# Attention: another order of query tiles and half-head preparation, one pool of three transpose banks, samples' scores half a quarter later

## The chip, the cores and the metric

The kernel runs on one core of one Trainium2 chip. The metric is device time in microseconds (us) of one execution. A run is timed several times and the median is given; beside it one execution is profiled, and its trace gives the engines' instructions with their start and length. The engines are PE (matrix), DVE (vector), ACT (scalar), POOL and SP; SP only issues transfers here. "Clock" is the granted clock of PE as a share of its full speed.

## What is computed

One layer of a streaming encoder for a prompt of 1024 tokens and for 8 samples of 16 tokens, each sample with its own 1024 cached keys and values.

```python
# prompt x (1, 1024, 1024), samples x (8, 16, 1024) with 1024 cached keys and values each
N_HEADS, HEAD_DIM, V_DIM, CHUNK = 4, 64, 128, 64          # a head has two maps of 64
h = rmsnorm(x, g_mix); z = h @ w_in
zq, zk, zv, zu = jnp.split(z, [QK_COLS, 2 * QK_COLS, 2 * QK_COLS + ATTN_WIDTH], axis=-1)
q, k = rmsnorm(zq per map, g_q), rmsnorm(zk per map, g_k)
k_all, v_all = concatenate([k_past, k]), concatenate([v_past, v])
def diff_attend(q, k, v, bias, mask, lam):
    s = jnp.einsum('bqhmd,bkhmd->bhmqk', q, k).astype(jnp.float32) * (HEAD_DIM ** -0.5)
    s = jnp.where(mask, s + bias[None, :, None], NEG_INF)
    p = jax.nn.softmax(s, axis=-1)
    w = p[:, :, 0] - lam * p[:, :, 1]
    return jnp.einsum('bhqk,bkhe->bqhe', w.astype(v.dtype), v)
# the prompt: block-causal, in query tiles of 128; the samples: 16 queries over 1024 + 16 keys.
# o is normalised per head, joined to the depthwise convolution's half (GLU, 31 taps, LayerNorm,
# swish) and projected by w_out; then memory cross-attention and an MLP of 4096, both with residuals
```

## The kernel before

All of the prompt's input projections come first, to about 293 us of the span. Then comes the **attention stage**, from the last `z` matmul at 293.0 us to 538.33 us, where the first matmul of the output projection `pj` starts. Cross-attention and the MLP follow. The change touches only the attention stage.

In the stage four generators, the streams, issue work and are woven into one program:

- `prompt_stream`: for each of 4 heads, 8 query tiles of 128 rows. `attend` computes a tile's scores. For each of two maps and each bank of 512 keys it issues two matmuls, one with the rounded queries `qs` (L674) and one with their rest `ql` (L675), into a bank `sc`. A reduction on DVE (L679) moves the bank to `p` and finds its extreme, ACT takes the exponential (L681), and DVE mixes both maps (L688). `values` transposes the mixed weights (`pT`, L699), copies them to `wT` (L701, in turn by ACT and DVE) and multiplies by the values into `po` (L704). Tile i has i + 1 blocks of 128 keys.
- `prep(h, c)` makes half c (512 rows) of head h ready: two loads `r`, four transposes of keys (`kst`, L619) and four of queries (`qst`), two copies by ACT and two by DVE that split keys into `kS` (L628, L629), and four and two for `qs`, `ql` (L639 to L641). Tile 0 to 3 of a head need half 0; tiles 4 to 7 need both halves' keys and half 1's queries.
- `sample_stream`: for each sample four quarters of 256 cached keys. For a quarter, eight transposes in two groups of four (two heads each, in the bank `kT`, L768), each group copied by ACT to `ku` (L770), then four score matmuls `ss` (L777), one for each head, on 32 columns of the array each. Then come the exponential `sp` (L800), the transposes `wt` (L810) and the values `spo` (L825), and ACT's copy `raw` (L830).
- `conv_norm` and `memory_stream`: the conv's normalisation (`cvt`, `cvT`) and the memory's keys and values (`memT`, `mk`, `mv`).

A program orders each engine's instructions when the kernel is built, by the streams' progress, by priorities and by its own estimate of when inputs are ready. On the chip each engine then runs its list in order. The eight PSUM banks are pools by tag: a transpose that takes a bank waits until the bank's last user has been read. The next stage's banks for `pj` take the place of the samples' banks, so `pj` starts only after the last sample. The prompt's last tiles may run beside it.

The lines that set the order before are these:

```python
PA = 3
PB1 = {"sc": 2, "tr": 2, "po": 1, "kT": 1, "ss": 1, "acc": 1}
if i % 4 == PA and n + 4 - PA < len(tiles):
    its.append(prep(tiles[n + 4 - PA][0], tiles[n + 4 - PA][1] // 4))
```

So the next half is prepared beside tile 3 (or 7), one tile ahead of its first use.

Of the kernel before, what the change touches and what calls it, by code (L numbers as in the profile page):

```python
# [10 lines left out]
F32 = mybir.dt.float32  # L11
R32 = mybir.dt.float32r
AF = mybir.ActivationFunctionType
ALU = mybir.AluOpType
# [26 lines left out]

EL = 3

PA = 3


NS, NL = 4, 3
# [6 lines left out]
TRS = ("tr", "sc", "tr", "sc", "kT", "sx")  # L54
WP, WS, WL, WM = (0, 1), (0, 1), (.2, .8), (.2, .8)
AB = {"rq": 2, "kS": 2, "rv": 4, "qs": 2, "p": (3, 1), "wT": 2}
PB1 = {"sc": 2, "tr": 2, "po": 1, "kT": 1, "ss": 1, "acc": 1}


def f32(ap):  # L60
# [4 lines left out]
def kernel(  # L65
# [489 lines left out]

    p2 = ExitStack()
    ppt = {}
    for nm, tags in (("ppsS", ("kT", "ss", "acc")), ("ppsP", ("sc", "tr", "po"))):
        pl = p2.enter_context(tc.tile_pool(name=nm, bufs=1, space=PSUM, reuse_waits="tile"))
        ppt.update({t: pl for t in tags})  # L560
    wlm = p2.enter_context(tc.tile_pool(name="wkM", bufs=1, side="right", reuse_waits="tile"))
# [60 lines left out]
    def prep_keys(h, c):  # L622

        ps = flipped(halves[1, h, c], f"kst{h}_{c}")
        kS = wk.tile([P, 2, 512], R32, name=f"kS{h}_{c}", tag="kS", bufs=AB["kS"])
        kSs.setdefault(h, []).append(kS)
        for m in range(2):
            act.copy(kS[HALF[m], m, :], ps[HALF[m]])  # L628
            dve.tensor_sub(kS[HALF[1 - m], m, :], ps[HALF[m]], f32(kS[HALF[m], m, :]))  # L629
        yield  # L630

    def prep_queries(h, c):

        ps = flipped(halves[0, h, c], f"qst{h}_{c}")
        qs = wk.tile([P, 2, 512], R32, name=f"qs{h}_{c}", tag="qs", bufs=AB["qs"])
        ql = qlow[c]
        for m in range(2):
            a, b = HALF[m], HALF[1 - m]
            act.activation(qs[a, m, :], ps[a], AF.Copy, scale=gqk[a])  # L639
            act.activation(qs[b, m, :], ps[a], AF.Copy, scale=gqk[a])  # L640
            dve.scalar_tensor_tensor(out=ql[a, m, :], in0=ps[a], scalar=gqk[a], in1=f32(qs[a, m, :]),  # L641
                                     op0=ALU.mult, op1=ALU.subtract)
        qss[h, c] = (qs, ql)
        yield
# [74 lines left out]
    def prompt_stream():  # L719
        for c in range(2):  # L720
            qlow.append((wk1 if c else wk).tile([P, 2, 512], R32, name=f"ql{c}", bufs=1))
            pool.memset(f32(qlow[c]), 0.0)
        tiles = [(h, i) for h in range(NH) for i in range(8)]
        yield from prep(0, 0)
        last = iter(())
        for n, (h, i) in enumerate(tiles):
            st = {}
            its = [attend(h, i, st), last]
            if i % 4 == PA and n + 4 - PA < len(tiles):
                its.append(prep(tiles[n + 4 - PA][0], tiles[n + 4 - PA][1] // 4))  # L730
            yield from alternate(*its)
            last = values(h, i, st["w"], st["s0"])
        yield from last
# [4 lines left out]
    def sample_setup():  # L738
        for wi in range(2):
            r = rpool.tile([P, 512], F32, name=f"n8_{wi}", tag="r")  # L740
            sp.dma_start(r, d8[wi])
            ps = bk("kT", f"t8_{wi}")
            for h in range(NH):
                pe.transpose(ps[:, h * P:(h + 1) * P], r[:, h * P:(h + 1) * P], ident)
            if wi:
# [6 lines left out]

    def sample_keys(b):

        pm = ws.tile([P, 1152], F32, name=f"sp{b}", tag="sp", bufs=2)
        mn = [3e38]
        for c in range(2):
            sb = bk("ss", f"ss{b}_{c}")
            for cc in range(2):
                if (b, 2 * c + cc) not in krs:  # L760
                    load_keys(b, 2 * c + cc)
                kr = krs[b, 2 * c + cc]
                u = ws.tile([P, NH, 256], F32, name=f"ku{b}_{c}_{cc}", tag="ku", bufs=UB)
                for hp in range(2):
                    ps = bk("kT", f"kT{b}_{c}_{cc}_{hp}")
                    for h in range(2):
                        for t in range(2):
                            pe.transpose(ps[:, h * 256 + t * P:h * 256 + (t + 1) * P],  # L768
                                         kr[:, t, (2 * hp + h) * P:(2 * hp + h + 1) * P], ident)
                    act.copy(u[:, 2 * hp:2 * hp + 2, :], ps.rearrange("p (h k) -> p h k", h=2))  # L770
                    yield
                with tc.high_priority(offset=TILED):

                    hs = (2, 3, 0, 1)
                    for n, h in enumerate(hs):
                        with tc.issue_after(lead) if n else ExitStack():
                            i = pe.matmul(sb[32 * h:32 * h + 32, cc * 256:cc * 256 + 256], zq[:, b, h, :], u[:, h, :],  # L777
                                          start=True, stop=True)
                        lead = lead if n else i.ins
                    sx["lead"] = lead  # L780
                if cc:
                    init, mn[0] = mn[0], sm(1, "smn", bufs=8)
                    add = biass if c else zero.broadcast_to([P, 512])
                    dve.tensor_tensor_reduce(out=pm[:, c * 512:(c + 1) * 512], in0=sb, in1=add, scale=1.0, scalar=init,
                                             op0=ALU.add, op1=ALU.min, accum_out=mn[0])
                yield
        sx["sc", b] = (pm, mn[0])

    def sample_weights(b):
# [44 lines left out]
    def sample_stream():  # L834
        sample_setup()
        yield from sample_keys(0)
        for b in range(8):
# [3 lines left out]
                continue  # L841

            vals = sample_values(b)
            for n, _ in enumerate(sample_keys(b + 1)):
                if n % 3 == 2:
                    next(vals)
                yield

# [815 lines left out]
```

## Time and profile before

| | |
|---|---|
| Median of 3 runs | 1572.34 us (1572.21 to 1577.45) |
| The profiled execution | 1569.38 us, of which the span is 1567.6 |
| PE busy in the span | 1496.2 us, 95% |
| DVE, ACT, POOL busy | 1094.0, 731.4, 297.8 us |
| Mean granted clock | 0.99 |
| Attention stage | 293.0 to 538.33 us of the span |

The profiled execution is 3.0 us under the median; 1.8 us of it lie outside the span. Times in rows count from the span's start. A row with "x4" stands for four records; a matmul of `po`, `ss` or `spo` leaves two records, one of `sc` or a transpose one. A busy share says how full an engine was, not that it was the limit; where PE sits idle, the row names the instruction whose end let it go on.

### The profile page before, as it was taken

What the parts mean: (1) busy time and instruction counts of PE and PEld (TensorE: products, weight loads), DVE (VectorE), ACT (ScalarE), POOL (GpSimd) and SP (SyncE); (2) the same over time, 40 slices, a digit from 0 to 9 for tenths busy, and PEclk for the clock granted to TensorE, in tenths of its full rate; (3) what the DMA queues carried; (4) which work ended last, traced back from release to release, by engine and by line L of the source; (5) the groups of instructions that cost most, each with busy time, mean ns of one, the idle gap of its engine ahead of it and who ended that gap; (6) DMA issues with size and microseconds to landing.
All of it is one profiled execution on the core that took longest, in us unless ns stands there. A gap on an engine that the chain in (4) does not pass through costs nothing.

```text
span 1567.6 us, 25652 instructions
## 1 busy us (share of the span) xinstructions
PE 1496.2 (95%) x9326; PEld 1293.3 (83%) x9326; DVE 1094.0 (70%) x1984; ACT 731.4 (47%) x1530; POOL 297.8 (19%) x410
## 2 busy tenths in 40 slices
PE   7999989888899899999999999999999999999999
PEld 7989787666677688886678999999999788878887
DVE  5999999975657754535758786666566556996565
ACT  6312011386777742634656454444353444544442
POOL 5354682032545330231011000000000000000000
PEclk9999999899999999999999999999999999999999
DMA  6423242567776553012422554443474567744443
GB/s 202 143 83 101 85 137 99 176 201 240 237 239 217 181 206 108 28 48 96 139 103 89 179 185 145 162 160 121 160 235 140 167 206 227 238 126 110 124 135 95
DMA packets 187122, 237.88 MB, mean 152 GB/s; under 512 B 23851, under 2 KB 101717, under 8 KB 186996
## 3 DMA queue, kind: packets, MB, share of 16 engines
q1 hardware_dynamic: 186996, 236.25, 47.2%
q8 instruction: 73, 1.20, 0.3%
q14 instruction: 53, 0.43, 0.1%
HBM read 172.59 MB, written 63.60 MB: 151 GB/s over the span
## 4 chain that ended last, share of the span: by engine, by line
PE 66%; DVE 7%; ACT 5%; DMA 5%; issue 2%; POOL 1%; SPq 0%; DVEq 0%; ACTq 0%; POOLq 0%
PE p L124 13%; PE p L123 13%; PE p L125 13%; PE pj L123 3%; PE pj L124 3%; PE pj L125 3%; DVE acc L307 1%; PE po L704 1%; PE q L124 1%; PE q L123 1%; PE q L125 1%; PE kT L768 1%; PE z L124 1%; PE z L125 1%; PE z L123 1%
## 5 line engine op out<-in xcount | busy, mean ns | idle before, releaser
L124 PE MATMUL p<-Bp,Ap 128*128 128x512 f32 x448 | 175.0, 391 | 1.1 <-DVE Bp L1532 1.1
L125 PE MATMUL p<-Bp,Ap 128*128 128x512 f32 x448 | 174.4, 390 | 0.0
L307 DVE SCALAR_TENSOR_TENSOR acc<-cp,wc,acc 128x1024 f32<-128x1024 f32 (+2 forms) x150 | 167.3, 1117 | 1.2
L123 PE MATMUL p<-Bp,Ap 128*128 128x512 f32 x448 | 158.1, 390 | 3.9 <-ACT Bp L1531 2.9
L1531 ACT CAST Ap<-w_xb 128x512 fp32r<-128x512 f32 x112 | 69.5, 621 | 161.8 <-PE p L125 131.7
L1532 DVE TENSOR_TENSOR Ap<-w_xb,Ap 128x512 fp32r<-128x512 f32 x112 | 76.9, 687 | 91.3 <-ACT Ap L1531 91.2
L123 PE MATMUL p<-b_t,s 128*128 128x288 f32 x384 | 114.5, 298 | 2.8 <-ACT s L1284 2.8
L124 PE MATMUL p<-b_t,s 128*128 128x288 f32 x384 | 114.4, 298 | 0.0
L125 PE MATMUL p<-b_t,s 128*128 128x288 f32 x384 | 113.9, 298 | 0.0
L123 PEld LDWEIGHTS p<-Bp,Ap 128*128 128x128 f32 x448 | 84.0, 188 | 22.3 <-ACT Bp L1531 3.8
L124 PEld LDWEIGHTS p<-Bp,Ap 128*128 128x128 f32 x448 | 84.1, 188 | 20.2 <-DVE Bp L1532 3.0
L125 PEld LDWEIGHTS p<-Bp,Ap 128*128 128x128 f32 x448 | 84.1, 188 | 17.4
L124 PE MATMUL z<-wqkv,h 128*128 128x512 f32 x216 | 85.7, 397 | 1.3 <-DVE wqkv L116 1.1
L123 PE MATMUL z<-wqkv,h 128*128 128x512 f32 x216 | 86.1, 399 | 0.0
L125 PE MATMUL z<-wqkv,h 128*128 128x512 f32 x216 | 85.4, 395 | 0.0
L123 PE MATMUL p<-b_b,a 128*128 128x288 f32 x256 | 75.9, 297 | 0.0
L124 PE MATMUL p<-b_b,a 128*128 128x288 f32 x256 | 75.7, 296 | 0.0
L125 PE MATMUL p<-b_b,a 128*128 128x288 f32 x256 | 75.6, 296 | 0.0
L123 PEld LDWEIGHTS p<-b_t,s 128*128 128x128 f32 x384 | 72.8, 190 | 3.3 <-ACT s L1284 3.3
L1368 ACT ACTIVATE o<-o 128x576 f32<-128x576 f32 x64 | 43.8, 685 | 68.1 <-DVE o L1378 29.2
L1051 DVE TENSOR_TENSOR XP<-pj,XP 128x512 f32<-128x512 f32 x54 | 37.1, 688 | 52.4 <-PE pj L125 52.2
L124 PEld LDWEIGHTS p<-b_t,s 128*128 128x128 f32 x384 | 73.0, 190 | 0.0
(513 smaller groups left out, 4315.9 us busy)
## 6 DMA issues: line engine op xcount, KB each, us to landing
kr<-in_cache_k_dram SPq DMA_DIRECT2D x32, 512.0 KB
vu<-in_cache_v_dram SPq DMA_DIRECT2D x32, 512.0 KB
w1t<-in_w_ff_dram SPq DMA_DIRECT2D x32, 512.0 KB
w_xb<-ds SPq DMA_DIRECT2D x64, 256.0 KB
da<-o SPq DMA_DIRECT2D x48, 256.0 KB
w_xb<-da SPq DMA_DIRECT2D x48, 256.0 KB
ds<-o SPq DMA_DIRECT2D x32, 256.0 KB
dxr<-XP SPq DMA_DIRECT2D x18, 256.0 KB
```

Of the source, the lines that this page charges most:

```text
L123: pe.matmul(out, lh, rh, start=first, stop=False)
L124: pe.matmul(out, lh, rl, start=False, stop=False)
L125: pe.matmul(out, ll, rh, start=False, stop=last)
L307: dve.scalar_tensor_tensor(out=out, in0=cp[:, lo + j:hi + j], scalar=wj, in1=out, op0=ALU.mult, op1=ALU.add)
L704: pe.matmul(po, wT[:, j * P:(j + 1) * P], vss[h][jb][:, j], start=4 * jb + j == 0, stop=4 * jb + j == i)
L768: pe.transpose(ps[:, h * 256 + t * P:h * 256 + (t + 1) * P], kr[:, t, (2 * hp + h) * P:(2 * hp + h + 1) * P], ident)
L1051: dve.tensor_add(xr[t][n], ps, xr[t][n])
L1368: act.activation(c, c, AF.Relu)
L1531: act.copy(u[:, 0], src)
L1532: dve.tensor_sub(u[:, 1], src, f32(u[:, 0]))
```

## The change

1. **Tiles.** Heads 0 to 2 take their query tiles in the order `QO` = 0, 1, 4, 5, 6, 7, 2, 3; head 3 keeps 0 to 7. Half 1 of a head is prepared beside its first tile, and half 0 of the next head beside the seventh in order. Buffers of `kS`, `qs` and `ql` go by the parity of head plus half, one each.
2. **Banks.** The bank `kT` is gone; `tr` has three banks in place of two, and the samples' key transposes take them too.
3. **Samples.** `sample_keys` issues a quarter's scores after the first group of the next quarter's transposes. The second group's copy is made by DVE in place of ACT (32 of 64 copies).

```diff
@@ -41,7 +41,7 @@
 EL = 3
-PA = 3
+QO = (0, 1, 4, 5, 6, 7, 2, 3)
@@ -54,7 +54,7 @@
 WP, WS, WL, WM = (0, 1), (0, 1), (.2, .8), (.2, .8)
 AB = {"rq": 2, "kS": 2, "rv": 4, "qs": 2, "p": (3, 1), "wT": 2}
-PB1 = {"sc": 2, "tr": 2, "po": 1, "kT": 1, "ss": 1, "acc": 1}
+PB1 = {"sc": 2, "tr": 3, "po": 1, "ss": 1, "acc": 1}
@@ -555,7 +555,7 @@
     p2 = ExitStack()
     ppt = {}
-    for nm, tags in (("ppsS", ("kT", "ss", "acc")), ("ppsP", ("sc", "tr", "po"))):
+    for nm, tags in (("ppsS", ("ss", "acc")), ("ppsP", ("sc", "tr", "po"))):
         pl = p2.enter_context(tc.tile_pool(name=nm, bufs=1, space=PSUM, reuse_waits="tile"))
         ppt.update({t: pl for t in tags})
@@ -622,7 +622,7 @@
         ps = flipped(halves[1, h, c], f"kst{h}_{c}")
-        kS = wk.tile([P, 2, 512], R32, name=f"kS{h}_{c}", tag="kS", bufs=AB["kS"])
+        kS = wk.tile([P, 2, 512], R32, name=f"kS{h}_{c}", tag=f"kS{(h + c) % 2}", bufs=1)
         kSs.setdefault(h, []).append(kS)
         for m in range(2):
@@ -632,8 +632,8 @@
         ps = flipped(halves[0, h, c], f"qst{h}_{c}")
-        qs = wk.tile([P, 2, 512], R32, name=f"qs{h}_{c}", tag="qs", bufs=AB["qs"])
-        ql = qlow[c]
+        qs = wk.tile([P, 2, 512], R32, name=f"qs{h}_{c}", tag=f"qs{(h + c) % 2}", bufs=1)
+        ql = qlow[(h + c) % 2]
         for m in range(2):
             a, b = HALF[m], HALF[1 - m]
@@ -720,14 +720,16 @@
             qlow.append((wk1 if c else wk).tile([P, 2, 512], R32, name=f"ql{c}", bufs=1))
             pool.memset(f32(qlow[c]), 0.0)
-        tiles = [(h, i) for h in range(NH) for i in range(8)]
+        tiles = [(h, i) for h in range(NH) for i in (QO if h < NH - 1 else range(8))]
         yield from prep(0, 0)
         last = iter(())
...
             st = {}
             its = [attend(h, i, st), last]
-            if i % 4 == PA and n + 4 - PA < len(tiles):
-                its.append(prep(tiles[n + 4 - PA][0], tiles[n + 4 - PA][1] // 4))
+            if n % 8 == 0:
+                its.append(prep(h, 1))
+            elif n % 8 == 6 and h < NH - 1:
+                its.append(prep(h + 1, 0))
             yield from alternate(*its)
             last = values(h, i, st["w"], st["s0"])
@@ -739,7 +741,7 @@
             r = rpool.tile([P, 512], F32, name=f"n8_{wi}", tag="r")
             sp.dma_start(r, d8[wi])
-            ps = bk("kT", f"t8_{wi}")
+            ps = bk("tr", f"t8_{wi}")
             for h in range(NH):
                 pe.transpose(ps[:, h * P:(h + 1) * P], r[:, h * P:(h + 1) * P], ident)
@@ -752,38 +754,52 @@
     def sample_keys(b):
+
         pm = ws.tile([P, 1152], F32, name=f"sp{b}", tag="sp", bufs=2)
-        mn = [3e38]
-        for c in range(2):
-            sb = bk("ss", f"ss{b}_{c}")
-            for cc in range(2):
-                if (b, 2 * c + cc) not in krs:
-                    load_keys(b, 2 * c + cc)
-                kr = krs[b, 2 * c + cc]
-                u = ws.tile([P, NH, 256], F32, name=f"ku{b}_{c}_{cc}", tag="ku", bufs=UB)
-                for hp in range(2):
-                    ps = bk("kT", f"kT{b}_{c}_{cc}_{hp}")
-                    for h in range(2):
-                        for t in range(2):
-                            pe.transpose(ps[:, h * 256 + t * P:h * 256 + (t + 1) * P],
-                                         kr[:, t, (2 * hp + h) * P:(2 * hp + h + 1) * P], ident)
-                    act.copy(u[:, 2 * hp:2 * hp + 2, :], ps.rearrange("p (h k) -> p h k", h=2))
-                    yield
-                with tc.high_priority(offset=TILED):
-
-                    hs = (2, 3, 0, 1)
-                    for n, h in enumerate(hs):
-                        with tc.issue_after(lead) if n else ExitStack():
-                            i = pe.matmul(sb[32 * h:32 * h + 32, cc * 256:cc * 256 + 256], zq[:, b, h, :], u[:, h, :],
-                                          start=True, stop=True)
-                        lead = lead if n else i.ins
-                    sx["lead"] = lead
-                if cc:
-                    init, mn[0] = mn[0], sm(1, "smn", bufs=8)
-                    add = biass if c else zero.broadcast_to([P, 512])
-                    dve.tensor_tensor_reduce(out=pm[:, c * 512:(c + 1) * 512], in0=sb, in1=add, scale=1.0, scalar=init,
-                                             op0=ALU.add, op1=ALU.min, accum_out=mn[0])
-                yield
+        mn, us, sbs = [3e38], [], []
+
+        def transposes(j, hp):
+            if (b, j) not in krs:
+                load_keys(b, j)
+            if not hp:
+                us.append(ws.tile([P, NH, 256], F32, name=f"ku{b}_{j}", tag="ku", bufs=UB))
+            ps = bk("tr", f"kT{b}_{j}_{hp}")
+            for h in range(2):
+                for t in range(2):
+                    i = pe.transpose(ps[:, h * 256 + t * P:h * 256 + (t + 1) * P],
+                                     krs[b, j][:, t, (2 * hp + h) * P:(2 * hp + h + 1) * P], ident)
+            (dve.tensor_copy if hp else act.copy)(us[j][:, 2 * hp:2 * hp + 2, :], ps.rearrange("p (h k) -> p h k", h=2))
+            return i.ins
+
+        def scores(j, lead):
+            c, cc = divmod(j, 2)
+            if not cc:
+                sbs.append(bk("ss", f"ss{b}_{c}"))
+            with tc.high_priority(offset=TILED):
+
+                for h in range(NH):
+                    with tc.issue_after(lead):
+                        i = pe.matmul(sbs[c][32 * h:32 * h + 32, cc * 256:cc * 256 + 256], zq[:, b, h, :], us[j][:, h, :],
+                                      start=True, stop=True)
+                    if not h:
+                        lead = i.ins
+            sx["lead"] = lead
+            if cc:
+                init, mn[0] = mn[0], sm(1, "smn", bufs=8)
+                add = biass if c else zero.broadcast_to([P, 512])
+                dve.tensor_tensor_reduce(out=pm[:, c * 512:(c + 1) * 512], in0=sbs[c], in1=add, scale=1.0, scalar=init,
+                                         op0=ALU.add, op1=ALU.min, accum_out=mn[0])
+
+        for j in range(4):
+            lead = transposes(j, 0)
+            yield False
+            if j:
+                scores(j - 1, lead)
+                yield True
+            lead = transposes(j, 1)
+            yield False
+        scores(3, lead)
+        yield True
         sx["sc", b] = (pm, mn[0])
@@ -841,8 +857,8 @@
             vals = sample_values(b)
-            for n, _ in enumerate(sample_keys(b + 1)):
-                if n % 3 == 2:
+            for scored in sample_keys(b + 1):
+                if scored:
                     next(vals)
                 yield
```

**Where instructions move.** The first place is PE where head 0 ends and head 1 begins: `sc_2`, `sc_3` and `sc_0` are scores of query tiles 2, 3 and 0, `r_1_0` a loaded half of head 1. Before:

```order
L768 MATMUL kT_0_0_0_4032<-ident,kr_0_4029 128x128 x4
L619 MATMUL qst_0_3509<-ident,r_1_0_3426 128x128 x4
L794 MATMUL ss_2_3885<-k_917,zq 32x128 x4
L582 MATMUL cvt_3524<-ident,al_3525 128x128 x4
L768 MATMUL kT_0_0_1_4072<-ident,kr_0_4029 128x128 x4
L674 MATMUL sc_0_0_0_3585<-kS_0_3435,qs_0_3514 128x128
L675 MATMUL sc_0_0_0_3585<-kS_0_3435,ql_2748 128x128
```

After:

```order
L675 MATMUL sc_3_1_0_3562<-kS_0_2758,ql_2747 128x512
L782 MATMUL ss_1_3272<-ku_3_3252,zq 32x256 x2
L582 MATMUL cvt_3356<-ident,al_3357 128x128 x4
L810 MATMUL ss_2_3411<-k_917,zq 32x128 x4
L704 MATMUL po_7_3302<-vr_0_2751,wT_7_0_3308 128x128 x4
L881 MATMUL memT_0_3376<-ident,mem_3374 128x128 x4
L881 MATMUL memT_1_3389<-ident,mem_3374 128x128 x4
L826 MATMUL wt_0_3440<-ident,sp_3063 128x128 x4
L619 MATMUL qst_0_3424<-ident,r_1_0_3312 128x128 x4
L826 MATMUL wt_4_3458<-ident,sp_3063 128x128 x4
L826 MATMUL wt_8_3515<-ident,sp_3063 128x128
L674 MATMUL sc_0_0_0_3609<-kS_0_3321,qs_0_3429 128x128
```

Before, the keys' transposes `kst` stand twenty rows above this piece, and no score of the prompt lies between them and `sc_0_0_0`. After, they stand just above the first row shown, and scores of tile 3 (`sc_3_1_0`) follow them, with only `qst` and other streams' pieces before `sc_0_0_0`.

The second place is PE at the end of the attention stage; `spo` on `v_918` is the last sample's last product. Before:

```order
L699 MATMUL pT_3_0_6142<-ident,p_3_0_6004 128x128 x4
L704 MATMUL po_2_6011<-vr_0_5568,wT_2_0_6016 128x128 x3
L825 MATMUL spo_6362<-vu_6_6429,wt_6298 32x128 x8
L825 MATMUL spo_6362<-v_918,wt_6298 32x128 x4
L674 MATMUL sc_4_1_0_6156<-kS_0_5575,qs_1_6079 128x512
L675 MATMUL sc_4_1_0_6156<-kS_0_5575,ql_2750 128x512
L674 MATMUL sc_4_1_1_6161<-kS_1_6044,qs_1_6079 128x128
L675 MATMUL sc_4_1_1_6161<-kS_1_6044,ql_2750 128x128
L123 MATMUL pj_0_6603<-wo_4_6565,MT_6552 128x512
L124 MATMUL pj_0_6603<-wo_4_6565,MT_6552 128x512
L123 MATMUL pj_0_6619<-wo_4_6565,MT_6552 128x512
L124 MATMUL pj_0_6619<-wo_4_6565,MT_6552 128x512
```

After:

```order
L699 MATMUL pT_7_1_6506<-ident,p_7_0_6417 128x128
L841 MATMUL spo_6362<-vu_6_6429,wt_6298 32x128 x8
L841 MATMUL spo_6362<-v_918,wt_6298 32x128 x4
L704 MATMUL po_7_6494<-vr_0_5524,wT_7_0_6500 128x128 x4
L704 MATMUL po_7_6494<-vr_1_5815,wT_7_1_6511 128x128 x4
L123 MATMUL pj_0_6603<-wo_4_6565,MT_6552 128x512
L124 MATMUL pj_0_6603<-wo_4_6565,MT_6552 128x512
L123 MATMUL pj_0_6619<-wo_4_6565,MT_6552 128x512
L124 MATMUL pj_0_6619<-wo_4_6565,MT_6552 128x512
```

Before, scores of head 3's tiles 4 and 5 stand around the first `pj`, and 24 score matmuls of its tiles 5 to 7, 26 transposes `pT` and 30 matmuls `po` of the prompt follow it. After, the prompt's last product `po_7` stands ahead of the first `pj`.

The third place is PE at a quarter's sample scores, early in head 1 (before, `ku_0_0` is a sample's quarter 0 and `kT_0_1` its quarter 1; after, `ku_3` is quarter 3). Before:

```order
L768 MATMUL kT_0_0_1_4587<-ident,kr_0_4574 128x128 x4
L699 MATMUL pT_3_0_4093<-ident,p_3_0_3896 128x128 x4
L674 MATMUL sc_4_0_0_4081<-kS_0_3435,qs_1_4020 128x512
L674 MATMUL sc_4_0_1_4086<-kS_1_3980,qs_1_4020 128x128
L675 MATMUL sc_4_0_0_4081<-kS_0_3435,ql_2750 128x512
L675 MATMUL sc_4_0_1_4086<-kS_1_3980,ql_2750 128x128
L810 MATMUL wt_0_4431<-ident,sp_4027 128x128 x4
L777 MATMUL ss_0_4573<-ku_0_0_4576,zq 32x256 x4
L768 MATMUL kT_0_1_0_4658<-ident,kr_1_4655 128x128 x4
L704 MATMUL po_3_4092<-vr_0_3428,wT_3_0_4098 128x128 x4
```

After:

```order
L769 MATMUL kT_3_1_3829<-ident,kr_3_3782 128x128 x4
L674 MATMUL sc_4_1_0_3895<-kS_0_3321,qs_1_3708 128x512
L674 MATMUL sc_4_1_1_3900<-kS_1_3667,qs_1_3708 128x128
L782 MATMUL ss_1_3798<-ku_3_3784,zq 32x256 x2
L841 MATMUL spo_3637<-vu_6_3871,wt_3439 32x128 x8
L841 MATMUL spo_3637<-v_918,wt_3439 32x128 x4
L675 MATMUL sc_4_1_0_3895<-kS_0_3321,ql_2747 128x512
L675 MATMUL sc_4_1_1_3900<-kS_1_3667,ql_2747 128x128
L598 MATMUL cvT_1_3835<-ident,xn_3371 128x128
L699 MATMUL pT_1_0_3889<-ident,p_1_0_3765 128x128 x2
L782 MATMUL ss_1_3798<-ku_3_3784,zq 32x256 x2
L598 MATMUL cvT_1_3835<-ident,xn_3533 128x128
```

Before, the four `ss` matmuls of a quarter stand together, right behind what precedes them. After, those of 19 of the 32 quarters are two and two, with full-width matmuls (here `spo`, then `sc`, `cvT` and `pT`) between them; none were so split before.

## Rows read from the trace of the kernel before

**Rows 1.** Windows: us, busy (count) of PE, PEld, DVE, ACT, POOL; PEclk, DMA share, GB/s
```profile
293.00:538.00 245.00, 210.91 (x2090) 167.11 (x2089) 166.62 (x437) 187.61 (x445) 95.28 (x159) 0.97 0.69 221
...
316.00:346.00 30.00, 26.01 (x264) 20.46 (x261) 22.95 (x64) 25.62 (x65) 11.16 (x26) 1.00 0.64 211
...
473.00:511.40 38.40, 37.45 (x400) 30.97 (x400) 26.75 (x70) 30.51 (x69) 19.34 (x29) 1.00 0.61 208
...
538.00:575.00 37.00, 36.95 (x196) 31.16 (x195) 26.16 (x59) 19.89 (x49) 14.97 (x20) 1.00 0.71 237
```

**Rows 2.** Waits of PE, 293 to 538 us: us in total, times, longest
```profile
PE sc L674 <- ACT qs L640: 4.7, 7, 1.3
PE ss L777 <- ACT ku L770: 4.6, 9, 0.9
PE wt L810 <- ACT sp L800: 3.5, 3, 1.7
...
PE kT L768 <- ACT ku L770: 2.4, 4, 0.8
...
PE sc L675 <- DVE ql L641: 1.8, 6, 0.5
...
PE pT L699 <- DVE ql L641: 0.6, 2, 0.5
```

**Rows 3.** Timeline of PE where head 0 ends: start, us, engine, line, operation, wait
```profile
346.08 0.48 PE L674 MATMUL sc<-kS,qs 128*128 128x512 f32 x1
...
361.71 0.80 PE L619 MATMUL kst<-ident,r 128*128 128x128 f32 x4
...
370.17 0.60 PE L619 MATMUL qst<-ident,r 128*128 128x128 f32 x4
...
372.58 0.33 PE L674 MATMUL sc<-kS,qs 128*128 128x128 f32 x1 [0.26 <-ACT qs L640]
```

**Rows 4.** Windows over the six longest score gaps; two of six, and their sum
```profile
346.10:372.60 26.50, 19.20 (x199) 13.36 (x196) 13.55 (x39) 16.64 (x41) 3.90 (x6) 0.87 0.67 222
...
496.40:511.40 15.00, 15.00 (x167) 13.47 (x167) 8.05 (x16) 10.58 (x23) 8.56 (x9) 1.00 0.42 143
sum 96.80, PE 83.02 PEld 67.98 DVE 52.40 ACT 69.09 POOL 35.05; mean PE 13.84 PEld 11.33 DVE 8.73 ACT 11.52 POOL 5.84
```

**Rows 5.** Timeline of PE in a stretch without waits
```profile
336.64 1.28 PE L704 MATMUL po<-vr,wT 128*128 128x128 f32 x10
337.68 0.42 PE L674 MATMUL sc<-kS,qs 128*128 128x384 f32 x1
...
338.11 0.39 PE L674 MATMUL sc<-kS,qs 128*128 128x512 f32 x1
...
338.58 0.60 PE L768 MATMUL kT<-ident,kr 128*128 128x128 f32 x4
339.01 0.82 PE L699 MATMUL pT<-ident,p 128*128 128x128 f32 x6
339.59 0.42 PE L674 MATMUL sc<-kS,qs 128*128 128x384 f32 x1
```

**Rows 6.** Timeline of PE around one quarter's sample scores
```profile
315.40 0.64 PE L777 MATMUL ss<-ku,zq 128*32 128x256 f32 x8 [0.42 <-ACT ku L770]
315.97 0.66 PE L768 MATMUL kT<-ident,kr 128*128 128x128 f32 x4
```

**Rows 7.** Groups by line and shape, 293 to 538 us: busy us, mean ns, idle before
```profile
L770 ACT COPY ku<-kT 128x512 f32<-128x512 f32 x64 | 37.3, 582 | 12.3 <-PE kT L768 12.1
...
L701 DVE COPY wT<-pT 128x512 f32<-128x512 f32 x9 | 6.2, 685 | 1.0 <-PE pT L699 0.9
```

**Rows 8.** Timeline of PE at the end of the attention stage
```profile
537.04 0.40 PE L825 MATMUL spo<-v,wt 128*32 128x128 f32 x8
537.37 0.50 PE L674 MATMUL sc<-kS,qs 128*128 128x512 f32 x1
...
538.33 0.50 PE L123 MATMUL pj<-wo,MT 128*128 128x512 f32 x1
```

## The prediction

> **What bounds the kernel now.** I read the windows first, because the change lies in one stage. The row of the whole stage [rows 1] shows PE 210.9 us busy in 245.0 us, 86%, at a clock of 0.97; DVE is 166.6 us busy (68%), ACT 187.6 (77%), and the transfers 69%. No engine is full, so waits in PE's list set the stage's length. Behind it, from 538 us on, PE is busy 36.95 of 37.0 us [rows 1]: there only the amount of PE work counts. So the time after can be put as one question: when does the first `pj` start, and how much of the prompt's work still stands behind it?
>
> The view of waits says where the stage's 34.1 us of idle PE time comes from. The change aims at two families of rows [rows 2]: scores and transposes that wait for the preparation of a half head (4.7 + 1.8 + 0.6 = 7.1 us), and samples' scores and transposes that wait for ACT's key copies (4.6 + 2.4 = 7.0 us). The rest (exponentials, mixes, the last values' load) is not touched directly.
>
> The timeline shows the first family at its largest [rows 3]. After the score at 346.08 no prompt score starts until 372.58, 26.5 us later: the keys of the next half are transposed at 361.71, its queries only at 370.17. But the windows over the six longest such gaps warn against taking their 96.8 us for a loss [rows 4]: PE is busy 83.0 of these, 86%, the same as outside them ((210.9 − 83.0) of (245.0 − 96.8), 86%), and in one of them, 15.0 of 15.0. The other streams fill them. Only 96.8 − 83.0 = 13.8 us of idle time lies there.
>
> **The change, part by part.**
>
> *The end of the stage.* After the change the tail of head 3 stands before the first `pj`: 24 score matmuls, 26 transposes and 30 `po` matmuls. Prices come from starts in a stretch without waits [rows 5]: a 512-wide score (338.58 − 338.11) / 2 = 0.235 us, a 384-wide one (338.11 − 337.68) / 2 = 0.215 at most, in proportion 0.176, a 256-wide one 0.118 likewise; a transpose (339.59 − 339.01) / 6 = 0.097; a `po` matmul, two records, 2 × (337.68 − 336.64) / 10 = 0.208. Twelve scores are 512 wide and four each 256, 384 and 512: 2.8 + 0.5 + 0.7 + 0.9 = 4.9 us. With 26 × 0.097 = 2.5 and 30 × 0.208 = 6.2 this makes 13.6 us. It is not new work: it leaves a place where PE is full. So `pj` may start at 538.3 + 13.6 = 551.9 (a stage of 258.9 us from 293.0) for no change in the total. If it is run at the stage's fill of 86% rather than at 100%, it costs 13.6 / 0.86 − 13.6 = **+2.2**; if it lies in what are waits now, 0. I take +2.2.
>
> *Half heads two tiles ahead.* Half 1 is prepared beside the first tile of a head and needed at the third, half 0 of the next head beside the seventh and needed two tiles on. A mean wait of this family is 0.67 us (4.7 / 7) [rows 2], a tile lasts several us, so all 7.1 us should go: **−7.1**. The other end is 0, if the queues of ACT and DVE make the copies late again. Sixteen loads of `r` move earlier on SP; no PE wait on `r` stands among the waits, so I price that at nothing; the cover is the tile between, and without it a load's landing would stand in the open. Other buffers by parity change no work.
>
> *Gaps that become shorter.* By the order, priced as above, the non-prompt work between the last score of one half and the first of the next falls from about 75 to 34 us. Of the 13.8 us idle there [rows 4], at most 6.7 are not in the family just counted. Since the gaps are no emptier than the rest, I take half: **−3.4** (0 to −6.7).
>
> *Samples' scores later, three banks.* A quarter's scores now have four transposes, 0.4 us [rows 5], and more between them and the last copy; the mean wait is 0.5 us (4.6 / 9) [rows 2]. That would remove it. But half the copies go to DVE, where a 512-wide copy takes 685 ns against ACT's 582 [rows 7], behind whatever DVE has queued, and `kT`'s banks are now shared with the prompt's transposes, so that a late reader of any stream holds up all. I take three fifths of 7.0: **−4.2** (0 to −7.0).
>
> *Split scores.* In the order, the four 32-column matmuls of 19 of the 32 quarters stand two and two, with full-width work between. The timeline prices a whole group at 315.97 − 315.40 = 0.57 us [rows 6]. One such matmul alone, two records of 256 columns, is twice a `po` matmul, 0.416 us; so four of them run side by side, and two parts cost at least 2 × 0.416 − 0.57 = 0.26 us more, at most another 0.57. 19 × 0.26 = **+5.0**, up to +10.8, and 0 where PE would have waited anyway. I take the lower price, since some of these places have waits.
>
> The Trainium skill, "TensorEngine Tiling (Array Packing)", Key Properties, says that changing the tiling mode drains the engine. That speaks against this change too: it makes 17 more runs of 32-column matmuls, 34 more changes of mode. This trace shows no separate drain: of a group's 0.57 us, 0.15 are left beyond one matmul's length, which bounds both changes of a run. By that rule with this bound the sum would be 17 × 0.15 = 2.6 us higher, and the result about −4 us.
>
> *No filler before `pj`.* From the last `spo` of the samples to `pj` four score matmuls ran, from 537.37 to 538.33 [rows 8]. In the new order nothing stands there: **+1.0** (0 to some us, if POOL and DVE are late with the operands of `pj`).
>
> *DVE and ACT.* DVE takes 32 × 0.685 = 21.9 us of copies and the tail's reductions, mixes and copies, estimated at 12 (twelve reductions, three mixes, a few copies at about 0.69 each): 166.6 + 21.9 + 12 = 200.5 us. ACT loses 32 × 0.582 = 18.6 us. At 258.9 us of stage that is DVE at 77%; I price it at nothing, because 30 us of the stage already hold it at 22.95 / 30.0 = 76.5% with PE 87% busy [rows 1]. If this cover fails, see the third rival.
>
> Sum: 2.2 − 7.1 − 3.4 − 4.2 + 5.0 + 1.0 = −6.5 us. Against the profiled execution's 1569.4 this makes 1562.9; against the median, 3.0 higher, 1565.8. I forecast **1566**, with `pj` starting near 538.3 + 13.6 − 6.5 = 545 us.
>
> **The rivals.**
>
> *Both chains loosen.* If the lists, with both families gone, run as the stretch from 473 to 511 us does, 37.45 busy of 38.4 (98%) [rows 1], the stage holds 210.9 + 13.6 + 5.0 = 229.5 us of work. At 95% that is 241.6 us, `pj` at 534.6, 17.3 us under the 551.9 of no change: 1555. It needs idle time to fall from 34 to 12 us. For it: both families are over 40% of the idle time, and later scores also give the exponential behind `wt` (3.5 us [rows 2]) other work to lie beside. Against it: the untouched rows alone are 20 us.
>
> *Nothing is won.* The key copies wait as long in DVE's queue as they did in ACT's, and the gaps' idle time only moves: without −4.2 and −3.4 the sum is +1.1, 1573. For it: the gaps are as full as the rest [rows 4]; against it: preparation two tiles ahead.
>
> *DVE becomes the bound (slower).* Each score bank is released by a DVE reduction, and now so are half of the key banks, in the one list of DVE. If waits on it keep DVE's share at or below 75%, the stage lasts 200.5 / 0.75 = 267.3 us, `pj` starts at 560.3, 8.4 us over 551.9: 1581. It decides from a share of 77% downwards; 70% would give 27 us more. For it: over the whole stage DVE stands at 68% now; against it: the 76.5% above, at which PE still had a higher fill than its mean.
>
> **How the numbers follow.** Chances: forecast (−1 to −12 us) 0.42, both chains loosen (beyond −12) 0.20, nothing won (−1 to +8) 0.18, DVE the bound (over +8) 0.20. A measurement of this kernel tells about 0.5%, 7.9 us, from no change. Nearly half of the forecast's own range lies beyond that, 0.20, so faster is 0.20 + 0.20 = 0.40, same 0.22 + 0.18 = 0.40, slower 0.20. The range leaves out about half of each outer case: 1550 (idle time down to 7 us) to 1582. The forecast's own range is 1560 to 1571.
>
> **What would show it.** In the profile after: waits of scores on `qs` and `ql` under 2 us in the stage (else the second step is wrong); waits of `ss` and `kT` on the key copies about 3 us, now on DVE more than on ACT; no score gap over 10 us between halves; two `ss` parts each 0.4 us or more from start to next start; PE in the stage at 90 to 92%; first `pj` near 545, and from there PE full, with only `pj` left. The prediction is wrong if `pj` starts past 552, with DVE over 75% and PE's waits put down to DVE copies, or before 536 with PE over 94%.

## The result: 1.6% slower

The changed kernel takes 1598.68 us (median of 4 runs, 1596.98 to 1600.21); the kernel before, with one more run on the same chip, 1574.89. The ratio is 1.0157, 95% interval 1.0138 to 1.0175, some 24 us. The forecast was 1566, its range ended at 1582, and slower had a chance of 0.20. None of the rivals described what happened. Two single executions, 3757 us in e3 and 5149 us in e15, took over twice as long as the others of their kernel and are left out of every number below.

The profiled execution took 1599.43 us with a span of 1597.6. The windows of the changed kernel (columns as in [rows 1]), the attention stage:

```profile
298.00:582.40 284.40, 244.93 (x2201) 188.46 (x2200) 202.68 (x515) 187.95 (x447) 101.73 (x173) 0.93 0.60 192
```

The stage is 284.4 us long against 245.3 before, 39.1 more, of which 13.6 are the prompt's last work, which now lies in it. So 25.5 us are lost in the stage. (It also starts 5 us later. Over all runs of this study, which don't touch what lies ahead of it, it starts anywhere between 292.7 and 298.1 us, so this is an execution's own spread; the profile of before happened to be 5.5 us under the median above.)

Where the 25.5 us went is best seen when a stage is cut in three: time in which PE is idle; PE time lost to the low clock (busy time times one minus the granted clock, summed over windows of 1 us); and the rest, PE's work at full clock.

| Version | Stage, us | PE idle | Lost to clock | Work at full clock |
|---|---|---|---|---|
| before | 245.3 | 34.1 | 6.8 | 204.4 |
| changed | 284.4 | 39.4 | 15.0 | 230.0 |

Work rises by 25.6: 13.6 is the prompt's tail, and the other 12 is new. Idle time rises by 5.3 and the clock's loss by 8.2. Together 25.5.

**The new work** is the split score groups. The timeline of the changed kernel shows the price of one part, two of the four matmuls:

```profile
465.28 0.63 PE L782 MATMUL ss<-ku,zq 128*32 128x256 f32 x4
465.84 0.33 PE L699 MATMUL pT<-ident,p 128*128 128x128 f32 x1
```

From its start to the next start this part of two takes 0.56 us, as long as a whole group of four (0.57 [rows 6]). 19 × 0.56 = 10.6 us. The Trainium skill, "TensorEngine Tiling (Array Packing)", Key Properties, says that tiles operate independently and in parallel; the trace agrees, since two more members cost 0.01 us.

**The waits** of PE in the changed kernel (columns as in [rows 2]):

```profile
PE memT L881 <- DVE kS L629: 3.7, 1, 3.7
PE sc L674 <- ACT qs L640: 3.5, 3, 1.6
PE qst L619 <- DMA r<-dq: 3.4, 1, 3.4
PE kT L769 <- ACT zt L604: 2.6, 1, 2.6
PE kT L769 <- DVE mem L134: 2.5, 1, 2.5
...
PE kT L769 <- DVE ku L771: 1.7, 4, 0.9
...
PE kst L619 <- DMA r<-dq: 1.2, 1, 1.2
```

The family of `ss` behind key copies is gone (4.6 in [rows 2]), and what the two families still hold has shrunk. New are waits of a transpose for a bank that another stream's tile holds (`memT` for `kS`, `kT` for `zt` and for `mem`), and waits on the loads `r`, of which there were none. The second kind stands at the stage's start:

```profile
306.69 0.63 PE L619 MATMUL kst<-ident,r 128*128 128x128 f32 x4 [1.21 <-DMA r<-dq]
...
313.29 1.09 PE L619 MATMUL qst<-ident,r 128*128 128x128 f32 x4 [3.42 <-DMA r<-dq]
```

Half 1 of head 0 is prepared beside the first tile, before its load has landed. What follows in the windows:

```profile
304.00:308.00 4.00, 2.61 (x22) 1.61 (x21) 3.90 (x5) 2.30 (x5) 0.00 (x0) 1.00 0.90 294
308.00:312.00 4.00, 0.67 (x2) 0.34 (x2) 3.87 (x7) 2.40 (x5) 0.19 (x1) 0.57 1.08 368
312.00:316.00 4.00, 2.71 (x15) 2.33 (x19) 2.57 (x7) 1.49 (x3) 0.00 (x0) 0.50 0.56 175
```

From 304 to 312 PE is busy 3.3 of 8 us; then its clock is at 0.50, the 1.2 GHz of its two levels, and it comes back only near 326. The stage of the changed kernel has five such places, the stage before had two.

### The profile page after: what moved, and what is told of

Same layout as the page of the kernel before. It is cut to its first block, busy times and chain, and to the rows that moved or that the text cites. A ratio compares the mean times of both kernels' runs of the same rounds, so it can differ in the third digit from the quotient of the medians.

```text
span 1597.6 us, 25645 instructions
## 1 busy us (share of the span) xinstructions
PE 1517.6 (95%) x9326; PEld 1301.3 (81%) x9326; DVE 1115.6 (70%) x2016; ACT 718.5 (45%) x1498; POOL 297.7 (19%) x410
## 4 chain that ended last, share of the span: by engine, by line
PE 66%; DVE 9%; DMA 6%; ACT 3%; issue 2%; POOL 1%; SPq 1%; DVEq 0%; ACTq 0%; POOLq 0%
PE p L125 12%; PE p L124 12%; PE p L123 12%; PE pj L123 3%; PE pj L125 3%; PE pj L124 3%; PE po L704 2%; PE ss L782 1%; DVE acc L307 1%; PE kT L769 1%; DMA w_xb<-ds 1%; PE q L124 1%; PE q L125 1%; PE q L123 1%; PE z L124 1%
```

## The experiments

Differences are medians against the kernel before on the same chip, in us; a ratio with its interval stands beside. In what follows, the *tail* is the prompt's work that stands behind the first `pj` in PE's list in the kernel before. The changed kernel's own difference by this measure is +23.8; a comparison with it goes by these differences, and by its interval it is good to some 3 us.

**One part alone, or left out.** The first theory, S, was that the shared banks tie streams together.

```diff
-PB1 = {"sc": 2, "tr": 2, "po": 1, "kT": 1, "ss": 1, "acc": 1}
+PB1 = {"sc": 2, "tr": 3, "po": 1, "ss": 1, "acc": 1}
...
-                    ps = bk("kT", f"kT{b}_{c}_{cc}_{hp}")
+                    ps = bk("tr", f"kT{b}_{c}_{cc}_{hp}")
```

That is e2. e1 has only the lines on `QO`, `prep` and the buffers by parity; e3 only `sample_keys` and its caller; e4 all but what e1 has; e8 all but what e2 has.

e1: 

> The kernel before with the first part alone: the order of tiles and the earlier preparation of half heads. Theory S (three shared banks make one stream's transposes wait for another stream's slow reader, and PE's clock falls behind each such wait): the part is harmless or gains, -8 to +3 us against the kernel before. Theory P (half 1 of head 0 is asked for before its loads have landed, and PE's list stands still behind it): +8 to +20 us. Theory D (the samples' new order with DVE copies and split scores costs the time): 0, -5 to +5 us.

Measured −0.2 (0.9998, 0.9982 to 1.0015): harmless, as S had it.

e2: 

> The kernel before with the second part alone: no bank of its own for the samples' key transposes, three shared ones for all. Theory S: +10 to +20 us, with waits of one stream's transposes on another stream's copies of 8 us or more. Theory P: 0 to +4 us. Theory D: 0 to +4 us.

Measured +13.6 (1.0084, 1.0057 to 1.0111). In size it is S's, but S asked for 8 us or more of waits on another stream's reader, and they come to 4.2 us at most.

e3: 

> The kernel before with the third part alone: samples' scores half a quarter behind, half of the key copies on DVE, with the bank of before. 7 of 32 score groups are split in the order. Theory D: +10 to +20 us. Theories S and P: -4 to +6 us, of which split groups cost 7 x 0.26 to 7 x 0.57 = 2 to 4 us.

Measured +6.6 (1.0042, 1.0026 to 1.0058).

e4: 

> The changed kernel with the first part undone: tiles and preparation as before, shared banks and the samples' new order as after. Theory S: still +15 to +25 us over the kernel before. Theory P: no more than +8 us. Theory D: +12 to +22 us.

Measured +20.3 (1.0127, 1.0102 to 1.0152): banks and samples add up, 13.6 + 6.6.

e8: 

> The changed kernel with the bank of its own for the samples' key transposes again (tr 2, kT 1); 7 score groups are split. If the parts add up (alone: tiles 0, banks +13.6, samples +6.8 us) and tiles cost 5 us only beside both others: +7 to +12 us over the kernel before, with PE idle 30 to 34 us in the stage. If three shared banks help once the tiles are in the new order: +15 us or more.

Measured +4.4 (1.0026, 1.0012 to 1.0040). Without the banks part, four fifths of the loss are gone.

**The split.**

```diff
-                for h in range(NH):
+                for n, h in enumerate((2, 3, 0, 1)):
...
-                    if not h:
+                    if not n:
                         lead = i.ins
```

e5: 

> The changed kernel with a quarter's four score matmuls issued in the order of heads 2, 3, 0, 1, so that the first of them waits for the later copy and no group of four is split in the list (19 of 32 are in the changed kernel). Theory G (each split costs a second group's length, 0.56 us from start to next start in the changed kernel's trace, all of it on PE's path): 19 x 0.56 = 10.6 us less than the changed kernel, +13 to +15 us over the kernel before. Rival (the two parts fill time in which PE would have waited for the second copy): 0 to -3 us, so +21 to +25 us over the kernel before.

Measured +11.3 (1.0070, 1.0044 to 1.0096), 12.5 us under the changed kernel: theory G, and a little more than its 10.6. The groups by line show it, the changed kernel first, then e5; the second number is the mean of one:

```profile
L782 PE MATMUL ss<-ku,zq 128*32 128x256 f32 x256 | 35.4, 414 | 0.0
```

```profile
L782 PE MATMUL ss<-ku,zq 128*32 128x256 f32 x256 | 26.6, 409 | 0.4 <-DVE ku L771 0.3
```

One record lasts the same; but PE's time under them falls by 8.8 us, because four run at once again. Work at full clock falls from 230.0 to 218.6, which is the 204.4 of before plus 13.6 of tail and 0.6. So the split is 11.4 us of work, and keeping the heads in the order of before takes it away at little cost in waits (idle PE time 39.9 us against 39.4).

**The start, the copies, the casts.**

```diff
-            if n % 8 == 0:
+            if n % 8 == (0 if h else 1):
...
-            (dve.tensor_copy if hp else act.copy)(us[j][:, 2 * hp:2 * hp + 2, :], ...)
+            act.copy(us[j][:, 2 * hp:2 * hp + 2, :], ...)
...
-        act.copy(u[:, 0, :n], raw[:, :n])
+        (cast or act.copy)(u[:, 0, :n], raw[:, :n])
```

The first is e6, the second e7, the third (with `cast=pool.tensor_copy` for the memory's weights) e11; e9 is e5 and e7 together, e10 all of e5 to e7.

e6: 

> The changed kernel with half 1 of head 0 prepared beside the second tile instead of the first; all other preparations as in the changed kernel. Theory L (at the stage's start the transposes of that half stand in PE's list before their loads have landed, 4.6 us of waits, and PE's clock stays low behind them): 4 to 7 us less than the changed kernel, +18 to +21 over the kernel before, with no wait of kst or qst on the loads of r over 1 us. Rival (the waits are only put down to another instruction, since DVE is 90% busy there): within 2 us of the changed kernel.

Measured +21.9 (1.0135, 1.0112 to 1.0158), 1.9 under the changed kernel, which is not clear of noise. The waits on `r` are gone from the list of waits, and PE's idle time falls from 39.4 to 34.8. So theory L's waits are real; that removing them wins its 4 to 7 us isn't shown.

e7: 

> The changed kernel with all 64 key copies on ACT as before; 21 score groups are split in the order. Theory V (DVE's list became the one that is waited for): 5 us or more under the changed kernel. Rival (DVE has room, and ACT is the list that is held up): 0 to +6 us over the changed kernel, +25 to +31 over the kernel before.

Measured +17.1 (1.0099, 1.0069 to 1.0128), 6.7 under the changed kernel, which spoke for V.

e9: 

> The changed kernel with scores unsplit (heads 2, 3, 0, 1) and all key copies on ACT; tiles, shared banks and the scores' delay stay. If the two effects add (the first took 15 us off, the second 9): 1574 us, +1 to +3 us over the kernel before. By the trace's parts (218 us of PE work at full clock, 32 us idle, 6 us lost to the clock, as the run with copies on ACT showed): a stage of 256 us against 259 for no change, -2 to -3 us. Rival (with the first quarter score waiting for a copy again, ACT's copies are waited for as before): +6 us or more, idle PE time of 38 us or more.

Measured +19.4 (1.0128, 1.0112 to 1.0143): the rival, and 8 us worse than e5 with its copies on DVE. Idle PE time is 46.6 us. What ACT's copies gave in e7 they took back here; V isn't shown.

e10: 

> As the run before this one in the list, and half 1 of head 0 prepared beside the second tile. If that step adds what it took off alone (4.6 us): 1 to 5 us under the kernel before. If the start only moves its waits: within 2 us of the version without it.

Measured +17.9 (1.0118, 1.0101 to 1.0136), 1.5 under e9: beside the other list the later start is worth little.

e11: 

> The changed kernel with the 16 casts of the memory's weights on POOL in place of ACT, so that nothing on ACT stands behind their loads; 16 score groups are split in the order (19 before, 1.8 us less). Theory H (ACT's list stands still for late loads, 20.6 us of waits on transfers in the changed kernel against 13.4 before; banks are read late, PE idles and its clock falls): 6 to 12 us less than the changed kernel. Rival (these waits lie beside others): no more than 3 us less.

Measured +18.7 (1.0128, 1.0104 to 1.0152), 5.1 under the changed kernel, of which 1.8 are three splits less: theory H (6 to 12) in part at most.

**Who shares a bank.** All three have the new tiles and unsplit later scores; e13 undoes the banks part, and e14 and e15 move tags between two banks and one.

```diff
 e14:
-                ps = bk("tr", f"cvt{t}")
+                ps = bk("kT", f"cvt{t}")
-                ps = bk("tr", f"cvT{g}_{ct}")
+                ps = bk("kT", f"cvT{g}_{ct}")
-                ps = bk("tr", f"memT{t}_{hf}")
+                ps = bk("kT", f"memT{t}_{hf}")
 e15: these, and
-            ps = bk("kT", f"kT{b}_{j}_{hp}")
+            ps = bk("tr", f"kT{b}_{j}_{hp}")
```

e13: 

> The changed kernel with scores unsplit and the samples' key transposes alone in a bank of their own (two others for all the rest). The same with three shared banks took +11 us over the kernel before, with 5.9 us of PE waits on readers of another stream's bank. Theory S (what is shared decides): -5 to +3 us, with under 3 us of such waits. Rival (once the groups are not split, shared banks cost nothing): +8 to +13 us.

Measured −2.0 (0.9993, 0.9980 to 1.0007): the own bank is worth 13.3 us here (e5 has +11.3), as much as e2 lost by giving it up.

e14: 

> As the run with the own bank, except that the conv's and the memory's transposes take that one bank too; the prompt has its two to itself. Theory S: the samples now wait for readers of the conv's and the memory's banks, +8 to +20 us over the kernel before, waits on another stream's readers 6 us or more. Rival (it is the prompt's and the samples' transposes that hinder each other): -5 to +4 us.

Measured +56.4 (1.0357, 1.0340 to 1.0374). One bank for three streams is far worse: PE is idle 63.7 us in the stage and loses 29.3 to the clock.

e15: 

> As the run with the own bank, except that the samples' key transposes share two banks with the prompt's, and the conv's and the memory's transposes have the single bank. Theory S in its general form (any sharing of the samples' bank costs): +8 to +20 us. If only the readers of the conv's and the memory's banks are slow: -5 to +4 us, with under 3 us of waits on another stream's readers.

Measured +16.8 (1.0113, 1.0088 to 1.0138).

So far all times agreed with S, though its waits did not. But in each version with a loss over 7 us the order of PE's list also had the whole prompt ahead of the first `pj`, and in the others not. The last two runs move only that.

**Only the tail.**

```diff
-    for nm, tags in (("ppsS", ("kT", "ss", "acc")), ("ppsP", ("sc", "tr", "po"))):
+    for nm, tags in (("ppsS", ("po", "ss")), ("ppsP", ("sc", "tr", "kT", "acc"))):
```

The banks of `pj` now take the place of the prompt's `po` and the samples' `ss`. For e17 this is done to the kernel before: PE's list is the same, row for row, up to the first `pj`, and then the tail comes first.

e17: 

> The kernel before with only the place of the banks changed: the next stage's banks for pj take the place of the prompt's po and the samples' ss, so that all of the prompt stands ahead of the first pj, as in every version with shared banks; up to there PE's list is that of the kernel before, row for row. If the place of the prompt's tail costs what shared banks cost: +10 to +16 us. If it costs little more than its work, which leaves a full stretch (13.6 us of work at the fill of the stage's end): +1 to +5 us.

Measured +17.3 (1.0099, 1.0073 to 1.0125). Windows of e17: the stage up to where `pj` started before, the stretch from there to the first `pj`, and what follows:

```profile
294.10:539.50 245.40, 215.24 (x2071) 170.33 (x2073) 166.37 (x437) 187.65 (x443) 95.34 (x158) 0.93 0.68 221
539.50:570.60 31.10, 21.16 (x139) 16.00 (x131) 22.86 (x52) 19.43 (x50) 14.87 (x21) 0.93 0.78 265
570.60:607.60 37.00, 37.00 (x163) 29.95 (x163) 10.74 (x15) 4.07 (x9) 3.72 (x4) 0.96 0.23 75
```

The first stretch is as long as the whole stage before, 245.4 us, and at its end PE stands in its list where the first `pj` came before, within 2 us (the last `spo` starts at 539.79). The tail, 13.6 us of work, then takes 29 us, from 541.64 on. Its timeline shows why: each tile's scores wait for a bank's reduction, its transposes for the mix, its products for the copy, and nothing of another stream is left to run between.

```profile
539.79 0.40 PE L825 MATMUL spo<-v,wt 128*32 128x128 f32 x8
...
541.64 0.50 PE L674 MATMUL sc<-kS,qs 128*128 128x512 f32 x1 [0.62 <-DVE mn L679]
...
555.02 1.60 PE L704 MATMUL po<-vr,wT 128*128 128x128 f32 x12 [1.30 <-ACT wT L701]
...
565.09 1.07 PE L699 MATMUL pT<-ident,p 128*128 128x128 f32 x8 [2.70 <-DVE p L688]
```

e18: 

> The version with the new tiles, unsplit later scores and the own bank (-2 us), with the same change of places, so that its prompt also ends ahead of the first pj as with three shared banks (+11 us). If sharing is what costs: +0 to +4 us over the kernel before. If the tail's place is what costs: +9 to +14 us.

Measured +21.2 (1.0129, 1.0105 to 1.0153), from −2.0 for e13. So a loss of S's size arises with no sharing at all, when the tail is put ahead. That doesn't refute S for the other versions: in e18 the last sample's product starts at 521.71 and `pj` at 572.45, so 51 us of the prompt stand alone, while in e5 the prompt and the samples end together. And e14, whose prompt is also ahead, lies 35 us above e18: what shares a bank can cost more than the tail's place.

**Looking for a better version.** e12 is the kernel before with the new tiles, e6's later start, unsplit later scores, ACT's copies and the own bank; e16 adds e11's casts.

e12: 

> The kernel before with the new tiles, half 1 of head 0 prepared beside the second tile, and the samples' scores half a quarter later but unsplit, with all copies on ACT, and the samples' own bank kept. From the run without shared banks (+4.4 us): 7 splits less at 0.6 us, 4 us, and 1 to 5 us for the copies and the start: 1 to 6 us under the kernel before. If shared banks are what the other steps need to pay: 0 to +5 us.

Measured −0.3 (1.0002, 0.9988 to 1.0015).

e16: 

> The kernel before with the new tiles, the first preparation later, unsplit later scores, all copies on ACT and the own bank, as in the run that came to -0.3 us, and the 16 casts of the memory's weights on POOL. If ACT's waits for late loads are still on the path: 3 to 8 us under the kernel before. If they lie beside other work: within 3 us of it.

Measured −4.4 (0.9966, 0.9948 to 0.9984): the fastest of all. Its stage is the shortest (224.7 us), and of the prompt 46 score matmuls and 47 `po` matmuls run beside `pj` (24 and 30 in the kernel before).

## Why the prediction was wrong

Two things sort the versions, and mostly they go together. Those with the whole prompt ahead of the first `pj` (the changed kernel, e2, e4 to e7, e9 to e11, e14, e15, e17, e18) lie between +11 and +56 us; those with a tail beside `pj` (e1, e3, e8, e12, e13, e16) between −4 and +7. In all of the first group but e17 and e18 the samples' key transposes also share banks with another stream; in none of the second. The cuts of a stage into parts, for some of them:

| Version | Stage, us | PE idle | Lost to clock | Work at full clock | Time |
|---|---|---|---|---|---|
| e2, shared banks alone | 272.3 | 40.7 | 13.5 | 218.1 | +13.6 |
| e13, own bank, tail beside `pj` | 239.2 | 33.6 | 6.6 | 199.0 | −2.0 |
| e5, shared banks, tail first | 269.0 | 39.9 | 10.6 | 218.6 | +11.3 |
| e18, own bank, tail first | 279.8 | 48.0 | 9.3 | 222.5 | +21.2 |
| e17, before, tail first | 276.5 | 40.1 | 16.2 | 220.1 | +17.3 |

Where in the stage the time is lost tells the two apart. Idle time and the clock's loss together, in us, in a stage's first 100 us, in its last 45 us, and in all of it (one profile each; up to the tail e17 has the list of before, and their first columns still differ by 3):

| Version | First 100 us | Last 45 us | Stage |
|---|---|---|---|
| before | 25.4 | 6.7 | 40.9 |
| changed | 30.8 | 6.9 | 54.4 |
| e2, shared banks alone | 36.6 | 4.9 | 54.2 |
| e5, shared banks, tail first | 32.3 | 6.1 | 50.5 |
| e13, own bank, tail beside `pj` | 24.3 | 7.1 | 40.3 |
| e17, before, tail first | 28.5 | 16.9 | 56.3 |
| e18, own bank, tail first | 23.3 | 19.2 | 57.3 |

The windows of the first and the last part, for before, e2 and e17, show the idle time and the mean clock:

```profile
293.00:393.00 100.00, 81.39 (x765) 62.32 (x764) 70.74 (x184) 73.60 (x180) 26.44 (x52) 0.91 0.70 225
493.30:538.30 45.00, 38.38 (x399) 30.97 (x397) 29.47 (x74) 36.21 (x90) 19.82 (x30) 1.00 0.45 151
```

```profile
294.05:394.05 100.00, 76.94 (x609) 61.64 (x609) 68.16 (x174) 67.07 (x166) 26.48 (x52) 0.81 0.58 183
521.30:566.30 45.00, 40.12 (x455) 30.87 (x455) 31.41 (x88) 33.75 (x87) 11.04 (x24) 1.00 0.40 137
```

```profile
294.10:394.10 100.00, 82.73 (x746) 61.99 (x745) 69.28 (x181) 71.79 (x176) 25.18 (x50) 0.86 0.68 222
525.60:570.60 45.00, 32.44 (x232) 25.04 (x231) 32.54 (x77) 31.00 (x77) 18.05 (x29) 0.88 0.61 208
```

1. **The banks: this step failed.** I priced three shared banks, together with the later scores, at −4.2, at worst 0, and the end of the stage, whose new order comes with them, at +2.2. The banks part alone costs +13.6 (e2), and in the new order 13.3 (e5 less e13). Of e2's 13.3 us of idle time and lost clock, 11.2 lie in the first 100 us, far from the tail. PE's waits there for the prompt's queries on ACT (`qs`) are 8.3 us, against 2.2 before. The longest of them, in e2, has a late load of a memory weight ahead of the query's copies in ACT's list:

```profile
370.79 0.62 ACT L113 CAST wmk<-wmk_3r 128x512 fp32r<-128x512 f32 x1 [3.17 <-DMA wmk_3r<-in_w_mk_dram]
371.43 0.68 ACT L639 ACTIVATE qs<-qst,gqk 64x512 fp32r<-64x512 f32 x1
...
372.86 0.80 PE L674 MATMUL sc<-kS,qs 128*128 128x128 f32 x2 [4.33 <-ACT qs L640]
```

   With the shared banks PE and ACT thus have another order of work, in which PE waits more at the stage's start. How much of the 13.6 is that order and how much is waiting for a shared bank isn't shown.

   **The end of the stage (+2.2)** is not where the changed kernel lost its time: its last 45 us lose 6.9 us, those of before 6.7. In it, as in e2 and e5, only the prompt's last eight `po` matmuls stand behind the last sample's product, so there is other work beside the tail, and the low price fits. Where the tail stands alone it doesn't: e17 and e18 measure +17.3 and 23.2 (from e13). Beside `pj`, where PE is full [rows 1], the same waits cost nothing.

2. **Split scores: mechanism right, size wrong.** I took the lower end, 5.0, because members run side by side. A part of two costs as much as four, so a split costs a whole group: 11.4 us of work, over the upper end that I had named (10.8). With e5 undoing it, idle time stays the same, so nothing of it filled waits.

3. **Half heads two tiles ahead (−7.1).** The waits on `qs` and `ql` fell from 7.1 to 3.8 us, but at the stage's start 4.6 us on the loads came in place of them. I had named that case ("without it a load's landing would stand in the open") and priced it at nothing, because no wait on `r` stood in the trace of before; there the load was asked for three tiles later. The whole part gives −0.2 alone (e1), where a wait of 2.1 us on `r` stands too.

4. **Later scores (in the −4.2).** The waits for key copies fell from 7.0 to 2.1, as I had said. In their place came waits for banks held by other streams, 11.6 us of them in the changed kernel against 2.1 before, counted from the view of waits.

5. **Gaps (−3.4).** I read 13.8 − 7.1 = 6.7 as the most that lies in the gaps beside the family already counted; it is the least, since not all of that family lies in gaps. There are still four prompt gaps of about 10 us or more, the longest 16.9. Together steps 3 to 5 gave nothing: idle PE time rose from 34.1 to 39.4.

6. **The clock was missing from the sum.** 8.2 us of the loss are work at the lower clock, behind new idle stretches; in e2, with banks alone, 6.7.

The two measured parts, 13.6 (e2) and 11.4 (split), make 25 us of a measured 24. The rival in which DVE becomes the bound is not what happened, though the time lies on its side: DVE is busy 71% of the stage, and taking all its key copies away gives −7 in one version (e7) and +8 in another (e9 against e5).

Open is what in the banks part costs: no version has shared banks with a tail beside `pj`, and none has the order of the shared-bank lists with a bank of its own. That shared banks put the prompt ahead because the samples' transposes fall behind the prompt's is argued from the order only. Open too is why ACT's copies help e7 and hurt e9; each edit makes a new list on every engine, and some 8 us between lists is what this study can't assign.

## What to carry to other kernels

Before pricing moved work at a stage's mean fill, ask what else is ready at that place. A dependent chain's last tiles are nearly free beside a full engine; with another stream beside them to the end they cost here about their own work; alone they took twice that. Matmuls that share the array by columns are better kept next to each other in the list: here a full-width instruction between them cost a whole group. A change of banks also changed the order of the engines' lists, so price it by what then stands behind late loads, not only by the waits that it removes. And when two things change together in all versions, an experiment that moves one of them shows what that one can cost, not what it did cost elsewhere; look in each trace for the place where the time is lost.

## What was not expected of the hardware

Two matmuls of 32 columns of the array take 0.56 us from start to next start where four take 0.57. A stretch of 8 us in which PE was busy 3.3 us was followed by some 14 us with the clock at or near the lower level, 1.2 GHz. One late load thus costs more than its wait, 4.6 us: in this place another 5.3 us of work were lost to the clock.
